# A list scheduler that breaks ties by a table, one number per operation

## The chip, the cores and the metric

The kernel runs on one core of a Trainium2 chip. The metric is the device time of one execution, in microseconds. The engines are named as in the profile: PE is TensorE (PEld its weight loads), DVE is VectorE, ACT is ScalarE, POOL is GpSimd, and SP is SyncE, whose queue issues nearly all DMAs.

## What is computed

A trunk of two layers on 256 tokens of 1024 features, in float32. Each layer normalises x, scales and shifts it by vectors that come from a condition c, mixes, and adds the gated result to x. The first mixer has three attentions whose results are summed under gates: over compressed keys, over selected blocks, and over a window; the second is causal attention.

```python
def reference(x, c, positions, ...):
    cos, sin = rope_tables(positions)
    cond = jax.nn.silu(c)
    for i in range(DEPTH):                      # 2
        shift, scale, gate = jnp.split(cond @ ada_w[i] + ada_b[i], 3, axis=-1)
        h = rms_norm(x, norm_g[i]) * (1 + scale[:, None, :]) + shift[:, None, :]
        y = nsa_mixer(h, ...) if i == 0 else moba_mixer(h, ...)
        x = x + gate[:, None, :] * y
    return x
# both mixers: h @ w_in, norm and rotary embedding of q and k, attention of 16 heads
# (4 of k and v, 64 wide), then (o * silu(z)) @ w_out
```

## The kernel before

The kernel doesn't issue its instructions where they are written. Proxies record each call (`record`): an operation has a number in the order of recording (`id`), an engine, the operations that it depends on, the tiles that it needs, a planned cost, and a `level`. Calls inside `plan.group()` are one operation. At the end `issue` runs a list schedule over the 2447 operations: for each engine it looks for the operation that can start first by the planned times, and issues instructions in the order in which they are picked. Every engine then runs its own instructions in that fixed order, each waiting for what it needs. So a planned time only decides an order.

Among operations of one engine that can start at the same planned time, the one with the smallest (`_rank`, `id`) is taken. The levels are FIRST_OF_ALL = -2 and URGENT = -1 (the norms and what the first products wait for), CHAIN = 0 (attention steps, loads and most else), and FILL = 1 (products with weights, and the splitting of weights). Matmuls that address a part of PE's array (`tile_position`) have rank TILED = -0.5 when the matmul before them was tiled as well. An operation of negative rank may also be taken when it is ready within 250 ns (`AHEAD`). DMAs are operations too: those on SP are recorded with level CHAIN, and a load can be picked as soon as its tag has a free buffer (`room`, `_safe`). There are twelve buffers `early` for the weights of the start, five `raw` for later ones.

Work: a float32 product is made of three fp32r matmuls, of high and low parts: ACT rounds a weight tile of 128 x 1024 to `hi`, DVE takes the rest to `lo`, and the activations stand in `HT` (for products with w_in) or in `qg` tiles (with w_out), split in the same way. `product` issues hi*hi, hi*lo and lo*hi, with 512 or 256 columns. At the start c and x are loaded; `condz` (from c) times `ada_w` in tiled matmuls gives scale and shift (`AB`); x is squared, scaled (`n_in`), transposed on PE, copied from PSUM (`n_out`), and scaled and shifted into `HT`. The first products are those of k and v, k-slice by k-slice, as the slices of HT come. Then come the rest of the first mixer's projections, the compressed keys (`hid`, `pcT`, `kcm`), the attention of eight pairs of heads (scores into `ps`, softmax on DVE and ACT, transposes, `values` in tiled matmuls) with the products of z beside it, the product with w_out, the second norm (`next_h`), and the same for the second mixer.

The last operations to be named in the prediction: 0 is the load of c on ACT's queue, 1 and 2 are the loads of the two halves of x on SP's queue, 22 and 23 the first two pieces of `ada_w` (shift and scale), 24, 25, 28 and 29 the first pieces of `nsa_w_in` (29 has 256 columns), 520 a weight of the compressed keys, 650 to 656 the DVE and ACT steps behind `hid`, and 693 and 694 the `hi` and `lo` of a weight tile that is split at the same time.

Of the kernel before, what the change touches and what calls it, by code (L numbers as in the profile page):

```python
# [36 lines left out]
TILED, LATER = -0.5, 0  # L37
SHORT_ROWS = 1.4
# [13 lines left out]
class Plan:  # L52
# [59 lines left out]
    def _new(self, engine):  # L112
        op = {"id": len(self.ops), "engine": engine, "calls": [], "deps": set(), "needs": set(), "cost": 0.0,
              "level": self.level, "end": None, "columns": 0.0}
        self.ops.append(op)
        return op
# [56 lines left out]
    def _cost(self, engine, method, args, kw, aps):  # L173
# [13 lines left out]
        if engine == "T":  # L187
            if method == "transpose":
                return 262.0 if aps[1].dtype == F32 else 180.0
            cols = free(aps[2])  # L190
            if aps[2].dtype == F32:
                m = free(aps[1])
                if "tile_position" in kw and m <= 64:
                    return max(cols * 4.28 * max(32, m) / P, 60.0)
                return 2 * max(cols * 2.14, 264.0)
            return max(cols * (1.07 if aps[2].dtype == F32R else 1.0), 264.0)
# [22 lines left out]
    @staticmethod  # L219
    def _rank(op, e, mode):  # L220

        if e == "T" and op["level"] >= 0 and op["mode"] and mode:
            return TILED
        if e == "T" and op["mode"] and op["level"] > 0:
            return op["level"] + LATER
        return op["level"]

    def issue(self, opening=()):

        ops = self.ops  # L230
        after = [[] for _ in ops]
        first, last = {}, {}
        for op in ops:
            op["wait"] = len(op["deps"])
            for d in op["deps"]:
                after[d].append(op["id"])
            for name in op["needs"]:
                self.tiles[name]["left"] += 1
                first.setdefault(name, op["id"])
                last[name] = op["id"]  # L240
        for t in self.tags.values():
            t.tiles = sorted((n for n in t.tiles if n in first), key=lambda n: first[n])
            for k, n in enumerate(t.tiles):
                self.tiles[n]["place"] = k
            t.first, t.last = [first[n] for n in t.tiles], [last[n] for n in t.tiles]
            t.alive = [[a for a in range(b + 1) if t.last[a] >= t.first[b]] for b in range(len(t.tiles))]
            assert all(len(a) <= t.bufs for a in t.alive), (t.name, max(map(len, t.alive)), t.bufs)
            t.given, t.early, t.done, t.known = set(), set(), set(), {}
        closed = {}
        for waiting, for_, call in opening:  # L250
# [4 lines left out]
        gates = [g for g in {id(g): g for g in closed.values()}.values()]  # L255

# [18 lines left out]
        for op in ops:  # L275
            op["at"] = 0.0
            if not op["wait"]:
                ready[op["engine"]].append(op)
        done = 0
        while done < len(ops):  # L280
            best = None
            for e, ops_e in ready.items():
# [4 lines left out]
                for op in ops_e:  # L287
# [12 lines left out]
                    found.append((t, self._rank(op, e, mode), op["id"], op))  # L300
# [10 lines left out]
            ready[e].remove(op)  # L311
            for n in op["needs"]:
                t = self.tiles[n]
                if t["slot"] is None:
                    tag = t["tag"]
                    gate = closed.get(tag.name)
                    if gate and not gate["called"]:
                        gate["called"] = True
                        gate["call"]()
# [37 lines left out]
            for a in after[op["id"]]:  # L357
# [3 lines left out]
                if not b["wait"]:  # L361
                    ready[b["engine"]].append(b)
            for method, args, kw in op["calls"]:
                r = getattr(self.engines[e], method)(*[self._real(a) for a in args],  # L364
                                                     **{k: self._real(a) for k, a in kw.items()})
            done += 1
        return max(clock.values())
# [1052 lines left out]
```

## Time and profile before

| what | us |
|---|---|
| three runs | 332.24, 332.68, 333.10 |
| median | 332.68 |
| span of the profiled execution | 329.4 |
| median less span | 3.28 |
| PE busy in the span | 315.2 |

The profiled execution has no time of its own beside its span in what the runs left; the median of the three runs stands 3.28 us over the span. The span runs from the first to the last instruction of the program. Busy times of PE are modelled at their ends: a matmul's row holds waits of the pipeline too, so a stretch in which PE is always busy need not be one in which it works at its full rate. All recorded instructions stand on one line, L364, where they are issued, so tiles tell them apart.

### The profile page before, as it was taken

Reading aid. Unit: us, or ns where it says so; the run is one execution under the profiler, and the core shown is the slowest. Engines: PE = TensorE matmul, PEld = TensorE weight load, DVE = VectorE, ACT = ScalarE, POOL = GpSimd, SP = SyncE. Lnnn points to the kernel's source line nnn. Section 1 sums busy time; section 2 is a strip of 40 time slices with the busy share of each in tenths; the row PEclk is TensorE's granted clock in tenths of the full one; section 3 lists DMA queues with packets and bytes.
Section 4 is the critical chain, followed back from the end, with each engine's and each line's share of the span. In section 5 each row is a group of like instructions: output and inputs, shape, how many; then the busy total and the mean of one; then the engine's idle time right before and its main releaser. Section 6 shows DMA issues by size and latency. Waiting matters only on the chain.

```text
span 329.4 us, 6082 instructions
## 1 busy us (share of the span) xinstructions
PE 315.2 (96%) x2183; PEld 252.8 (77%) x2183; DVE 241.3 (73%) x581; ACT 199.9 (61%) x476; POOL 26.1 (8%) x98
## 2 busy tenths in 40 slices
PE   1989999999989999999999999998999999999995
PEld 1856766888668788768897578866788998989884
DVE  3352543887699899639998665998599999974754
ACT  5542250762674798556776774698565897965420
POOL 7000008950000000000000000000000000000000
PEclk9999999999999999999999999999999999999999
DMA  8998999029896809738455799626386413033102
GB/s 254 336 357 299 375 363 332 5 80 278 271 337 217 290 29 314 262 91 357 129 215 182 243 307 317 209 64 199 119 258 181 141 64 129 0 102 103 54 32 96
DMA packets 43738, 65.80 MB, mean 200 GB/s; under 512 B 3786, under 2 KB 20537, under 8 KB 43708
## 3 DMA queue, kind: packets, MB, share of 16 engines
q1 hardware_dynamic: 43540, 65.36, 60.1%
q8 instruction: 17, 0.28, 0.3%
q14 instruction: 13, 0.11, 0.1%
q10 hardware_dynamic: 168, 0.06, 0.1%
HBM read 64.36 MB, written 1.05 MB: 199 GB/s over the span
## 4 chain that ended last, share of the span: by engine, by line
PE 89%; DVE 3%; ACT 2%; issue 0%; ACTq 0%
PE ps L364 51%; PE acc L364 38%; DVE lo L364 1%; ACT HT L364 1%; DVE rs L364 1%; ACT n_out L364 0%; ACT n_in L364 0%; ACT hi L364 0%; DVE g L364 0%; DVE HT L364 0%; DVE y L364 0%; DVE pcT L364 0%; DVE X L364 0%; ACT pcT L364 0%; DVE n_in L364 0%
## 5 line engine op out<-in xcount | busy, mean ns | idle before, releaser
L364 DVE TENSOR_TENSOR lo<-raw,hi 128x1024 fp32r<-128x1024 f32 (+1 forms) x50 | 59.2, 1186 | 21.4 <-ACT hi L364 21.2
L364 ACT CAST hi<-raw 128x1024 fp32r<-128x1024 f32 (+1 forms) x50 | 51.0, 1025 | 34.5 <-PE acc L364 18.5
L364 PE MATMUL acc<-hi,HT 128*128 128x512 f32 (+1 forms) x176 | 54.1, 382 | 1.3 <-ACT HT L364 0.7
L364 PE MATMUL acc<-HT,hi 128*128 128x256 f32 x256 | 54.3, 297 | 0.0
L364 ACT ACTIVATE p<-ps,tiny 128x128 f32<-128x128 f32 (+1 forms) x96 | 39.5, 433 | 13.6 <-DVE tiny L364 13.4
L364 PEld LDWEIGHTS acc<-HT,hi 128*128 128x128 f32 x256 | 40.9, 189 | 1.4 <-issue 0.9
L364 PEld LDWEIGHTS acc<-hi,HT 128*128 128x128 f32 x176 | 32.0, 188 | 8.5 <-ACT HT L364 1.5
L364 PE MATMUL acc<-HT,lo 128*128 128x256 f32 x128 | 36.7, 287 | 0.0
L364 PE MATMUL acc<-lo,HT 128*128 128x512 f32 (+1 forms) x88 | 33.5, 388 | 0.2 <-DVE lo L364 0.2
L364 DVE TENSOR_REDUCE tiny<-ps 128x2 f32<-128x512 f32 (+2 forms) x40 | 24.8, 630 | 10.0 <-PE ps L364 9.5
L364 PE MATMUL ps<-KTA,qg 128*128 128x256 f32 (+1 forms) x192 | 31.0, 296 | 0.2 <-ACT pcT L364 0.2
L364 PEld LDWEIGHTS ps<-KTA,qg 128*128 128x128 f32 x192 | 25.9, 190 | 4.1 <-issue 2.2
L364 PE MATMUL ps<-hi,HT 128*128 128x512 f32 (+1 forms) x96 | 28.7, 365 | 0.0
L364 PEld LDWEIGHTS acc<-HT,lo 128*128 128x128 f32 x128 | 24.2, 189 | 0.5 <-issue 0.4
L364 ACT COPY pT<-ps 128x384 f32<-128x384 f32 x48 | 21.7, 490 | 3.7 <-PE ps L364 2.9
L364 PE MATMUL ps<-hi,qg 128*128 128x256 f32 (+1 forms) x96 | 23.7, 321 | 0.0
L364 PE MATMUL acc<-hi,qg 128*128 128x512 f32 x64 | 22.2, 397 | 0.0
L364 PE MATMUL ps<-identF,p 128*128 128x128 f32 x144 | 21.5, 275 | 0.0
L364 ACT ACTIVATION_READ_ACCUMULATOR p<-ps,tiny 128x1 f32 x96 | 20.7, 215 | 0.0
L364 PEld LDWEIGHTS acc<-lo,HT 128*128 128x128 f32 x88 | 16.5, 188 | 5.0 <-DVE lo L364 1.1
L364 PEld LDWEIGHTS ps<-hi,HT 128*128 128x128 f32 x96 | 17.1, 188 | 4.1 <-issue 1.6
L364 PE MATMUL ps<-pT,VA 128*64 128x256 f32 (+1 forms) x192 | 18.9, 334 | 0.0
(199 smaller groups left out, 576.4 us busy)
## 6 DMA issues: line engine op xcount, KB each, us to landing
raw<-in_ada_w_dram SPq DMA_DIRECT2D x32, 512.0 KB, 4.8
raw<-in_moba_w_in_dram SPq DMA_DIRECT2D x20, 512.0 KB, 4.0
early<-in_ada_w_dram SPq DMA_DIRECT2D x16, 512.0 KB, 6.8
early<-in_nsa_w_in_dram SPq DMA_DIRECT2D x12, 512.0 KB, 8.7
raw<-in_nsa_w_in_dram SPq DMA_DIRECT2D x12, 512.0 KB, 4.6
raw<-in_nsa_cmp_w_dram SPq DMA_DIRECT2D x8, 512.0 KB, 6.6
raw<-in_nsa_w_out_dram SPq DMA_DIRECT2D x8, 512.0 KB, 5.8
raw<-in_moba_w_out_dram SPq DMA_DIRECT2D x8, 512.0 KB, 3.6
```

Of the source, the lines that this page charges most:

```text
L364: r = getattr(self.engines[e], method)(*[self._real(a) for a in args], **{k: self._real(a) for k, a in kw.items()})
```

## The change

The diff adds a table `TURNS` with one number for each of the 2447 operations, a permutation of 0 to 2446 indexed by the operation's number. The list schedule takes (`_rank`, turn) in place of (`_rank`, number), and all levels above 0 rank as 0. The planned durations of some matmuls change: fp32r products, float32 matmuls, and transposes of 16-bit or fp32r tiles. The schedule is split into `_prepare`, `_order` and `issue`, which by itself changes nothing in what is issued. No operation is added or removed, and the buffers are the same. The table is cut to its first four lines here.

```diff
--- before.py
+++ after.py
@@ -1,3 +1,4 @@
+import collections
 from contextlib import ExitStack, contextmanager
 
 import concourse.bass as bass
@@ -35,6 +36,128 @@
 
 TICK = 10240 / 3
 TILED, LATER = -0.5, 0
+TURNS = [
+    153, 132, 129, 88, 134, 157, 243, 380, 730, 202, 247, 2134, 2043, 1895, 1989, 1464, 1700, 1836, 2107, 352, 282,
+    112, 8, 136, 138, 118, 140, 142, 160, 100, 705, 687, 121, 539, 114, 469, 331, 693, 920, 936, 1244, 1406, 883, 429,
+    526, 742, 574, 600, 1057, 783, 869, 1146, 711, 810, 1130, 774, 905, 533, 908, 1144, 843, 1284, 1152, 492, 1137,
+    1206, 189, 602, 152, 547, 468, 1107, 2241, 2109, 2251, 1794, 1763, 1527, 1788, 2093, 1986, 2242, 1561, 1854, 1652,
...
+    2426, 2442, 2387, 2444, 2430, 2417, 2432, 2425, 2416, 2428, 1147, 1451, 270,
+]
 SHORT_ROWS = 1.4
 ISSUE, FIRST_BYTE, RATE, LANDED = 450.0, 1500.0, 330.0, 700.0
 
@@ -111,7 +234,7 @@
 
     def _new(self, engine):
         op = {"id": len(self.ops), "engine": engine, "calls": [], "deps": set(), "needs": set(), "cost": 0.0,
-              "level": self.level, "end": None, "columns": 0.0}
+              "level": self.level, "end": None}
         self.ops.append(op)
         return op
 
@@ -186,14 +309,14 @@
         n = max(free(a) for a in aps)
         if engine == "T":
             if method == "transpose":
-                return 262.0 if aps[1].dtype == F32 else 180.0
+                return 262.0 if aps[1].dtype == F32 else 204.0
             cols = free(aps[2])
             if aps[2].dtype == F32:
                 m = free(aps[1])
                 if "tile_position" in kw and m <= 64:
-                    return max(cols * 4.28 * max(32, m) / P, 60.0)
-                return 2 * max(cols * 2.14, 264.0)
-            return max(cols * (1.07 if aps[2].dtype == F32R else 1.0), 264.0)
+                    return max(cols * 4.05 * max(32, m) / P, 60.0)
+                return 2 * max(cols * 2.05, 264.0)
+            return max(cols * 1.07 + 9.0 if aps[2].dtype == F32R else cols, 268.0)
         if engine == "A":
             return 0.833 * n + (51.0 if psum else 94.0) + 93.0 * sum(isinstance(kw.get(k), bass.AP) for k in ("bias", "scale", "accum_out"))
         if engine == "G":
@@ -221,21 +344,19 @@
 
         if e == "T" and op["level"] >= 0 and op["mode"] and mode:
             return TILED
-        if e == "T" and op["mode"] and op["level"] > 0:
-            return op["level"] + LATER
-        return op["level"]
-
-    def issue(self, opening=()):
+        return min(op["level"], 0)
+
+    def _prepare(self, opening):
 
         ops = self.ops
-        after = [[] for _ in ops]
+        self.after = [[] for _ in ops]
         first, last = {}, {}
+        self.uses = collections.Counter()
         for op in ops:
-            op["wait"] = len(op["deps"])
             for d in op["deps"]:
-                after[d].append(op["id"])
+                self.after[d].append(op["id"])
             for name in op["needs"]:
-                self.tiles[name]["left"] += 1
+                self.uses[name] += 1
                 first.setdefault(name, op["id"])
                 last[name] = op["id"]
         for t in self.tags.values():
@@ -245,14 +366,26 @@
             t.first, t.last = [first[n] for n in t.tiles], [last[n] for n in t.tiles]
             t.alive = [[a for a in range(b + 1) if t.last[a] >= t.first[b]] for b in range(len(t.tiles))]
             assert all(len(a) <= t.bufs for a in t.alive), (t.name, max(map(len, t.alive)), t.bufs)
+        self.opening = opening
+
+    def _order(self):
+
+        ops = self.ops
+        for op in ops:
+            op["wait"], op["at"] = len(op["deps"]), 0.0
+        for name, t in self.tiles.items():
+            t["left"], t["slot"], t["end"] = self.uses[name], None, 0.0
+        for t in self.tags.values():
+            t.free, t.next = [(0.0, k) for k in range(t.bufs)], 0
             t.given, t.early, t.done, t.known = set(), set(), set(), {}
         closed = {}
-        for waiting, for_, call in opening:
+        for waiting, for_, call in self.opening:
             left = sum(len(self.tags[f].tiles) for f in for_)
             gate = {"left": left, "for": set(for_), "end": 0.0, "call": call, "called": False}
             for w in waiting:
                 closed[w] = gate
         gates = [g for g in {id(g): g for g in closed.values()}.values()]
+        steps = []
 
         def room(name):
 
@@ -273,11 +406,9 @@
         tally, mode = {}, None
         ready = {e: [] for e in self.engines}
         for op in ops:
-            op["at"] = 0.0
             if not op["wait"]:
                 ready[op["engine"]].append(op)
-        done = 0
-        while done < len(ops):
+        while len(steps) < len(ops):
             best = None
             for e, ops_e in ready.items():
                 if not ops_e:
@@ -297,7 +428,7 @@
                         t = max(t, r)
                     if blocked:
                         continue
-                    found.append((t, self._rank(op, e, mode), op["id"], op))
+                    found.append((t, self._rank(op, e, mode), op["turn"], op))
                     first = t if first is None else min(first, t)
                 pick = min(found, key=lambda f: f[:3]) if found else None
                 if pick:
@@ -309,6 +440,7 @@
                     best = pick + (e,)
             start, _, _, op, e = best
             ready[e].remove(op)
+            opens = []
             for n in op["needs"]:
                 t = self.tiles[n]
                 if t["slot"] is None:
@@ -316,7 +448,7 @@
                     gate = closed.get(tag.name)
                     if gate and not gate["called"]:
                         gate["called"] = True
-                        gate["call"]()
+                        opens.append(gate["call"])
                     slot = min(tag.free)
                     tag.free.remove(slot)
                     t["slot"] = slot[1]
@@ -354,17 +486,28 @@
                         if t["tag"].name in g["for"]:
                             g["left"] -= 1
                             g["end"] = max(g["end"], t["end"])
-            for a in after[op["id"]]:
+            for a in self.after[op["id"]]:
                 b = ops[a]
                 b["at"] = max(b["at"], end if e == b["engine"] == "T" else seen)
                 b["wait"] -= 1
                 if not b["wait"]:
                     ready[b["engine"]].append(b)
+            steps.append((op, opens))
+        return max(clock.values()), steps
+
+    def issue(self, opening=()):
+
+        self._prepare(opening)
+        for op in self.ops:
+            op["turn"] = TURNS[op["id"]] if TURNS else op["id"] + 10000 * max(op["level"], 0)
+        end, steps = self._order()
+        for op, opens in steps:
+            for call in opens:
+                call()
             for method, args, kw in op["calls"]:
-                r = getattr(self.engines[e], method)(*[self._real(a) for a in args],
-                                                     **{k: self._real(a) for k, a in kw.items()})
-            done += 1
-        return max(clock.values())
+                getattr(self.engines[op["engine"]], method)(*[self._real(a) for a in args],
+                                                            **{k: self._real(a) for k, a in kw.items()})
+        return end
 
     def _real(self, a):
```

## Rows read from the trace of the kernel before

**Rows 1.** The page: the span, its first part (busy time of each engine, share of the span, instructions), and of its second part the line of what the DMA engines moved in each of 40 equal slices of 8.2 us.
```profile
span 329.4 us, 6082 instructions
...
PE 315.2 (96%) x2183; PEld 252.8 (77%) x2183; DVE 241.3 (73%) x581; ACT 199.9 (61%) x476; POOL 26.1 (8%) x98
...
GB/s 254 336 357 299 375 363 332 5 80 278 271 337 217 290 29 314 262 91 357 129 215 182 243 307 317 209 64 199 119 258 181 141 64 129 0 102 103 54 32 96
```

**Rows 2.** Busy time in stretches of 10 us. Columns: the stretch, its length, then busy us and instructions of PE, PEld, DVE, ACT and POOL, the granted clock of TensorE, the DMA share and GB/s.
```profile
0.00:10.00 10.00, 2.92 (x12) 2.59 (x13) 4.80 (x25) 4.40 (x7) 6.08 (x33) 1.00 0.86 271
10.00:20.00 10.00, 9.80 (x85) 7.39 (x84) 3.96 (x10) 6.49 (x10) 0.00 (x0) 1.00 1.12 338
20.00:30.00 10.00, 9.11 (x76) 5.75 (x74) 3.24 (x8) 1.11 (x2) 0.00 (x0) 1.00 0.94 321
...
90.00:100.00 10.00, 9.18 (x49) 6.79 (x46) 9.90 (x33) 6.20 (x10) 0.00 (x0) 1.00 0.92 316
...
220.00:230.00 10.00, 8.99 (x42) 6.43 (x42) 9.39 (x22) 8.64 (x24) 0.00 (x0) 1.00 0.50 158
...
320.00:330.00 10.00, 5.75 (x37) 5.00 (x35) 4.47 (x8) 0.00 (x0) 0.00 (x0) 0.95 0.25 92
sum 330.00, PE 315.23 PEld 252.81 DVE 241.27 ACT 199.91 POOL 26.14; mean PE 9.55 PEld 7.66 DVE 7.31 ACT 6.06 POOL 0.79
```

**Rows 3.** The chain that ended last, in stretches where PE is fed. Columns: start in us, how long, whose work, how many instructions (x24 on `ps` are matmuls with 256 columns, x12 on `acc` with 512).
```profile
208.55 2.84 PE ps L364 x24
211.40 2.79 PE acc L364 x12
```

**Rows 4.** The same chain in the attention of the first mixer. The `ps` pieces of two and three instructions are transposes or other matmuls of 110 ns.
```profile
138.02 1.38 PE acc L364 x12
139.40 0.86 PE ps L364 x2
140.25 0.35 PE acc L364 x3
140.61 0.33 PE ps L364 x3
...
158.33 0.36 PE acc L364 x3
158.69 0.52 PE ps L364 x2
```

**Rows 5.** Instructions in order of time around two holes of PE. Columns: start, how long, engine, line, operation, tile written and tiles read, shapes, count, and in brackets the idle time before it and what ended it.
```profile
91.66 0.49 PE L364 MATMUL acc<-hi,HT 128*128 128x512 f32 x1 [0.59 <-ACT n_in L364]
92.39 0.51 PE L364 MATMUL acc<-lo,HT 128*128 128x512 f32 x1 [0.23 <-DVE lo L364]
...
224.26 0.40 PE L364 MATMUL acc<-hi,HT 128*128 128x512 f32 x1
225.66 0.75 PEld L364 LDWEIGHTS ps<-identF,n_in 128*128 128x128 f32 x6 [1.44 <-DVE n_in L364]
```

**Rows 6.** In order of time, the first issues of SP's queue (SPq; the duration is that of issuing).
```profile
0.80 0.85 SPq L364 DMA_DIRECT2D X<-in_x_dram  x2
1.69 1.78 SPq L364 DMA_DIRECT2D early<-in_ada_w_dram  x2
4.35 2.54 SPq L364 DMA_DIRECT2D early<-in_nsa_w_in_dram  x2
```

**Rows 7.** DMA issues by line: how many, KB each, median us from issue to landing.
```profile
X<-in_x_dram SPq DMA_DIRECT2D x2, 512.0 KB, 4.5
```

**Rows 8.** In order of time, what stands before the first product: the load of `c`, `condz` made from it, the second half of the scaled x, its copy from PSUM, HT, and the first product.
```profile
0.79 0.59 ACTq L364 DMA_DIRECT2D rot<-in_c_dram  x1
...
4.99 0.17 DVE L364 TENSOR_TENSOR condz<-sg,RT 128x8 f32<-128x8 f32 x1
...
9.59 0.48 DVE L364 TENSOR_SCALAR n_in<-X,rs 128x512 f32<-128x512 f32 x1
...
12.77 1.07 ACT L364 COPY n_out<-ps 128x512 f32<-128x512 f32 x2 [0.83 <-PE ps L364]
...
15.56 0.60 ACT L364 ACTIVATE HT<-n_out,AB 128x256 fp32r<-128x256 f32 x1 [0.18 <-DVE AB L364]
...
16.21 0.73 PE L364 MATMUL acc<-hi,HT 128*128 128x512 f32 x2 [0.20 <-ACT HT L364]
```

**Rows 9.** In order of time, PE's first and last stretch of tiled matmuls (`condz` with 32 columns of weights, `pT` with 64) and two between, with what follows them.
```profile
10.63 1.51 PE L364 MATMUL ps<-early,condz 128*32 128x128 f32 x16
...
272.42 0.87 PE L364 MATMUL ps<-pT,VA 128*64 128x256 f32 x8
273.23 0.97 PE L364 MATMUL ps<-identR,n_parts 128*128 128x128 f32 x9
...
288.78 1.52 PE L364 MATMUL ps<-pT,VA 128*64 128x256 f32 x16
290.23 0.74 PE L364 MATMUL ps<-KTA,qg 128*128 128x256 f32 x4
...
297.00 0.87 PE L364 MATMUL ps<-pT,VA 128*64 128x256 f32 x8
```

115 rows, old and new, of the table TURNS are left out of this document.

## The prediction

> **What bounds the kernel now.** I read the page first. TensorE (PE) is busy 315.2 us of a span of 329.4 us, 96%, VectorE (DVE) 73%, ScalarE (ACT) 61% [rows 1]. The change issues the same instructions, so PE's own work stays: what an order can win is PE's idle time, and waits that hide inside "busy" rows. The Trainium skill (Perfetto Trace Analysis, Identifying the Most-Contended Engine) says that matmul busy share is a poor measure of TensorE's headroom and that the LDWEIGHTS share should be taken; by that share, 77% here, 76 us would be open instead of 14. The sum below goes by idle time and by measured waits instead.
>
> The stages show where the idle time lies [rows 2]. Of 14.2 us (329.4 - 315.2), 7.08 fall in the first 10 us, before loads have landed, and 3.65 after the last matmuls (9.4 - 5.75: the last eviction, the update of X, the store). An order of ready work hardly reaches the latter. In between stand 0.20 and 0.89 us in 10 to 30, 0.82 in 90 to 100, 1.01 in 220 to 230, and 0.53 in all other stages together (the rest of 14.2). So at most 3.5 us of visible idle time is open.
>
> Then the chain that ended last, for what "busy" hides. Where PE is fed, 12 matmuls with 512 columns take 2.79 us (232 ns each) and 24 with 256 columns 2.84 us (118 ns) [rows 3]. In the attention stages the same chain shows steps that cost more than their work: three transposes take 0.33 us there, so two should take 0.22, but take 0.86 at 139.40 and 0.52 at 158.69 [rows 4]: 0.64 and 0.30 us of waiting inside a busy engine, 0.47 on average. Attention fills eleven of the 10-us stages (120 to 190 and 260 to 300). At one such wait for each, an estimate, 5.2 us are hidden there.
>
> **The change, part by part.**
>
> (1) The durations of TensorE. No instruction comes or goes; they only move the planner's clock. A 512-column matmul goes from 228 to 232 ns (547.8 and 556.8 cycles at 2.4 GHz), which is what the chain shows [rows 3]. Cost nothing by itself; it makes the plan's times for PE truer.
>
> (2) Rank. All levels from 0 up now count as 0, so a product (FILL) and an attention step (CHAIN) that could start at the same time are told apart by the table. Read against the operations, the table still puts PE's attention steps (mostly under 1000) before its products (mostly 1300 to 2400), and ACT's and DVE's weight splits late (693 and 694 have 2290 and 2403). So chain before fill stays the rule, and what changes is the order among chain steps and among products. Negative levels still come before everything.
>
> (3) The start. This is where the table visibly moves something. All loads into free buffers are ready at once on SP, so their turns are their order. Now SP issues X (two halves), then the two ada_w pieces, then weights [rows 6]. By the table (operation numbers count from 0): 22 (ada_w, turn 8), 29 (w_in, 256 columns, 100), 25 (w_in, 118), then X (2 and 1: 129 and 132), then 23 (the other ada_w piece, 136). X is put behind 0.52 + 0.26 + 0.52 = 1.3 MB, and the second ada_w piece behind 0.78 MB more than now. At the 254 and 336 GB/s of the first two slices [rows 1] X lands 3.9 to 5.2 us later and that piece 2.3 to 3.1 us later. Now X is issued at 0.80 and lands 4.5 us later, at 5.3 [rows 6, 7]; the second half of the scaled x is done at 10.07 and its copies from PSUM end at 13.84, HT starts at 15.56 and the first product at 16.21 [rows 8]. The stretch from landing to 10.07 is 4.8 us of squares and small DVE steps; with transposes and two copies at about 0.55 us each right behind, an estimate of 7.0 us to the end of the copies. So X later by 4.4 gives copies at 5.3 + 4.4 + 7.0 = 16.7, and with HT (0.6) the first product at about 17.4, 1.2 later than now. If the ada_w piece decides instead, the first tiled matmuls (10.63 now [rows 9]) and all behind them shift by up to 3.1. Below nothing is excluded for this term: no input of the first product that decides lands earlier. I take +1.2, ends 0 and +3.1. From 30 us on PE shows no idle time, so such a delay reaches the end, less what 10 to 30 absorbs (next term). On ACT's queue c goes from first to third, some 0.6 us later for each load ahead (its own issue takes 0.59 [rows 8]); condz is made from it at 4.99 now and first used at 10.63 [rows 8, 9], so 5 us cover it: nothing. Without that cover it would cost 1.2 us.
>
> (4) The idle 1.09 us of 10 to 30 us [rows 2]. Weights now land before they can be used, so that PE should go on without a hole once started. I take half, -0.5; ends 0 and -1.1.
>
> (5) The other idle time, 2.36 us (0.82, 1.01, 0.53). At 91.66 and 92.39 PE waits for an eviction and a weight split [rows 5], and that split stands behind the chain of the compressed keys on DVE in the new table as well (2403 against 398 to 797). At 224 it runs dry while the small steps of the second norm end [rows 5], which have negative levels and which the table doesn't reach. So I take a quarter, -0.6; ends 0 and -2.4. What comes late next at both places is the same split on DVE.
>
> (6) The tiled matmuls (those that address a part of the array). There are 54 groups in the code and I count 32 stretches, from 10.63 to 297.00 [rows 9]. Eight matmuls take 0.81 us (272.42 to 273.23), sixteen in one stretch 1.45 (288.78 to 290.23), so joining two stretches saves 0.17 us and splitting one costs it. The planner still prefers a tiled group right after another. Two or three more joins, -0.4; ends +0.8 (five splits) and -1.7 (ten joins).
>
> (7) The hidden waits, 5.2 us. The table can reach these, since it sets which product stands between two steps of a chain. But many of them end with ACT or DVE, whose work and planned durations are unchanged and which are 61 and 73% busy, in bursts. I take 40%, -2.1; ends 0 and -5.2.
>
> (8) Order on SP and POOL behind the start: POOL works 26.1 us in all [rows 1], most of it early, and nothing is queued long behind it. On SP later loads change places too (520, a weight of the compressed keys, has 291 where those behind it have 251 to 264), but five buffers let only the next few go ahead. Cost nothing, hidden by products of the pieces already in. If a piece came late, its product would wait as at 92.39, 0.2 us; this lies within the ends of (5).
>
> **Sum:** +1.2 - 0.5 - 0.6 - 0.4 - 2.1 = -2.4 us. Against the profiled execution: span 329.4 - 2.4 = 327.0, and the 3.3 us that lie around it (median 332.68 less span) stay: 330.3 us, 0.7% below the median.
>
> **The rivals.**
>
> *The start costs more than the order wins (slower).* Place: the first product on HT. X and the second ada_w piece land later by the loads put before them, and PE has nothing else. Price: +3.1, and half of the gains of (4) to (7), -1.8: 334.0. It decides once the first product starts later than about 19.3 us. For it: SP's order in the table, and a PE without idle time afterwards to absorb it. Against it: 1.7 us of slack between the copies of x (13.84) and HT (15.56) now [rows 8]. Chance 0.19.
>
> *Tiled groups are torn apart (slower).* If the turns put products between groups, all 22 joins of now are lost: 22 x 0.17 = 3.7 us, and with the rest of the sum 332.7 - 2.0 + 3.7 = 334.4. Against it: the rank for tiled groups stays. The Trainium skill (TensorEngine Tiling, Key Properties) says that a change of tiling mode drains the array; the 0.17 us agree with it in sign. Chance 0.04.
>
> *No change that can be told.* The table only speaks among operations that can start at the same time, and chain stays before fill; a PE that is 96% busy then does the same work in another order, and waits move rather than go. The start and the hidden waits cancel: 332.7. Chance 0.16.
>
> *Much more goes.* Of the 10.4 us that all bounds of (4) to (7) hold together, 60% goes and the start costs nothing: 332.7 - 6.2 = 326.5. For it: the waits are many and small, which order can fill. Against it: DVE's bursts. Chance 0.18.
>
> **How the numbers follow.** The forecast has 0.43. A difference of 0.3%, 1.0 us, is about what a measurement here can tell from none. Faster: 0.43 + 0.18, less a little of the forecast's near side, 0.60. Same: 0.16 and that little, 0.17. Slower: 0.23. The range goes from the large gain, 326.5, to the late start with fewer gains than above (3.1 - 1.2: 334.6); outside it lie the rest of both ends, 2 in 10.
>
> **What the changed profile would show.** (3) SP's first load is ada_w, X lands at about 9.7 us, and the first product on HT starts at about 17.4. Right if 16.2 to 18; the first rival if over 19.3. (4) PE idle in 20 to 30 us under 0.5. (5) The holes at 90 and at 224 still there, somewhat shorter. (6) About 30 tiled stretches. (7) Fewer steps of two matmuls that take over 0.5 us in attention; the stages from 30 us to the end shorter by about 3. PE's busy time should fall with the span, since hidden waits lie in it. What would make it wrong: a first product that starts no later than now, or a total that moves through idle time that I count as out of reach, the first 10 us or the tail.

## The result and the profile after

The changed kernel takes 327.51 us (median of 4 runs, 327.35 to 328.55) against 332.81 us of the kernel before (4 runs, 332.24 to 333.10). The ratio is 0.9861, interval 0.9834 to 0.9889: 1.4% faster. The profiled execution of after has a span of 325.8 us and a time of its own of 327.62, so 1.82 us lie around its span. Before's later executions, with time and span side by side, have 2.0 to 2.1 us around it (332.04 with 330.0, 331.69 with 329.6), and spans from 329.2 to 332.1. The profiled one of before, 329.4, is at the low end of these, so the spans differ by 3.6 us and the medians by 5.3. The two traces explain the 3.6.

The page of after answers [rows 1]. PE's busy time fell with the span, by 3.0 us; the engine is still busy for 96%.

```profile
span 325.8 us, 6076 instructions
...
PE 312.2 (96%) x2183; PEld 251.5 (77%) x2183; DVE 241.9 (74%) x581; ACT 199.9 (61%) x476; POOL 26.5 (8%) x98
...
GB/s 235 330 358 364 361 371 287 13 115 320 277 250 259 272 199 179 325 312 231 171 125 152 249 333 240 256 66 141 118 256 160 165 67 66 129 66 68 63 0 129
```

The stages of after, columns as in [rows 2]. PE starts later (1.98 us busy in the first ten instead of 2.92) and then has no idle time at all from 10 to 30. The hole at 90 is gone and another stands at 80 to 90 (0.69). At the second norm 1.16 us are idle in 210 to 230 (1.27 in before).

```profile
0.00:10.00 10.00, 1.98 (x16) 1.52 (x18) 2.60 (x9) 3.87 (x5) 6.06 (x33) 1.00 0.79 260
10.00:20.00 10.00, 10.00 (x86) 8.38 (x84) 6.93 (x26) 6.59 (x13) 0.00 (x0) 1.00 1.13 333
20.00:30.00 10.00, 10.00 (x81) 6.73 (x78) 2.91 (x8) 2.19 (x4) 0.00 (x0) 1.00 1.08 364
...
80.00:90.00 10.00, 9.31 (x70) 7.27 (x66) 5.37 (x12) 7.86 (x15) 0.00 (x0) 1.00 0.91 294
90.00:100.00 10.00, 9.98 (x53) 6.87 (x52) 9.61 (x29) 5.04 (x9) 0.00 (x0) 1.00 0.81 259
...
210.00:220.00 10.00, 9.48 (x43) 6.72 (x42) 8.54 (x22) 8.68 (x22) 0.00 (x0) 1.00 0.20 63
220.00:230.00 10.00, 9.36 (x44) 6.86 (x43) 7.13 (x19) 6.83 (x17) 0.00 (x0) 1.00 0.53 158
```

The start of after in order of time answers [rows 6] and [rows 8]: two kinds of weights are issued ahead of X; two weight tiles are split (`hi`, `lo`) while X is still landing; the squares wait for X at 9.18 and 10.52; the copies end at 16.65; HT starts at 16.68. One more tiled stretch stands ahead of the first product at 17.95.

```profile
0.79 0.42 SPq L508 DMA_DIRECT2D early<-in_ada_w_dram  x1
1.27 1.09 SPq L508 DMA_DIRECT2D early<-in_nsa_w_in_dram  x2
3.70 1.49 SPq L508 DMA_DIRECT2D X<-in_x_dram  x2
...
6.46 0.60 ACT L508 CAST hi<-early 128x512 fp32r<-128x512 f32 x1
7.92 1.04 ACT L508 CAST hi<-early 128x1024 fp32r<-128x1024 f32 x1 [0.86 <-DMA early<-in_nsa_w_in_dram]
8.54 1.83 DVE L508 TENSOR_TENSOR lo<-early,hi 128x512 fp32r<-128x512 f32 x2
9.18 1.06 ACT L508 ACTIVATE n_in<-X 128x1024 f32<-128x1024 f32 x1 [0.21 <-DMA X<-in_x_dram]
...
15.57 1.08 ACT L508 COPY n_out<-ps 128x512 f32<-128x512 f32 x2 [0.97 <-PE ps L508]
16.68 0.60 ACT L508 ACTIVATE HT<-n_out,AB 128x256 fp32r<-128x256 f32 x1
16.95 1.07 PE L508 MATMUL ps<-early,condz 128*32 128x128 f32 x16
17.95 0.50 PE L508 MATMUL ps<-hi,HT 128*128 128x512 f32 x1
```

**Where the 3.6 us went.** Both kernels issue the same matmuls, so they can be compared at equal work. I give each matmul the duration that the changed planner has for it (293.1 us in all), and take the time at which a given amount of it has been started, less that amount: the time lost by then. Each difference between two columns is what is lost in between. The point of 8 us of work is passed at about 21 us, 40 at about 57, 80 at about 100, 200 in the second norm.

| us of work done | 8 | 20 | 40 | 80 | 200 | all |
|---|---|---|---|---|---|---|
| before | 12.42 | 15.30 | 17.84 | 21.44 | 29.99 | 32.46 |
| after | 13.81 | 14.59 | 16.67 | 19.71 | 27.17 | 28.86 |
| after less before | +1.39 | -0.71 | -1.17 | -1.73 | -2.82 | -3.60 |

So after stands 1.4 us behind at first and gets 2.1 us back at once; then it wins 0.5 us each from 20 to 40 and from 40 to 80, 1.1 up to the second norm (0.4 of it in the hole before that norm's transposes) and 0.8 in the second mixer. A single pair of profiles gives such a column only roughly: e10 and e11 below have the same two orders with one buffer more, and their last row would be +2.1, 0.0, -0.4, -1.8, -2.7, -3.0. What holds in both pairs is the 2.1 us between 8 and 20.

What it gets back at once is seen in the order of time of PE in before, at 20 to 24 us: after a tiled stretch PE has nothing until DVE has copied `row`, and the products in hand end before the second slice of HT is there.

```profile
20.45 1.07 PE L364 MATMUL ps<-early,condz 128*32 128x128 f32 x16
21.92 0.38 PE L364 MATMUL ps<-selP,row 128*128 128x2 f32 x2 [0.39 <-DVE row L364]
...
23.37 0.50 PE L364 MATMUL acc<-hi,HT 128*128 128x512 f32 x1 [0.50 <-ACT HT L364]
```

In after a product stands behind that stretch while the row is copied, and more products behind `selP`, all on weights that are split already. Nothing waits:

```profile
19.54 1.07 PE L508 MATMUL ps<-early,condz 128*32 128x128 f32 x16
20.54 0.51 PE L508 MATMUL acc<-lo,HT 128*128 128x512 f32 x1
21.00 0.38 PE L508 MATMUL ps<-selP,row 128*128 128x2 f32 x2
21.25 0.47 PE L508 MATMUL acc<-hi,HT 128*128 128x512 f32 x1
21.56 0.40 PE L508 MATMUL acc<-lo,HT 128*128 128x512 f32 x1
```

### The profile page after: what moved, and what is told of

Same layout as the page of the kernel before. It is cut to its first block, busy times and chain, and to the rows that moved or that the text cites. A ratio compares the mean times of both kernels' runs of the same rounds, so it can differ in the third digit from the quotient of the medians.

```text
span 325.8 us, 6076 instructions
## 1 busy us (share of the span) xinstructions
PE 312.2 (96%) x2183; PEld 251.5 (77%) x2183; DVE 241.9 (74%) x581; ACT 199.9 (61%) x476; POOL 26.5 (8%) x98
## 4 chain that ended last, share of the span: by engine, by line
PE 91%; DMA 3%; ACT 2%; DVE 2%; ACTq 1%; issue 1%; SPq 0%
PE ps L508 53%; PE acc L508 37%; DMA raw<-in_nsa_w_in_dram 2%; DMA y<-in_nsa_cmp_pe_dram 1%; ACTq L508 1%; ACT n_out L508 1%; DVE rs L508 1%; ACT HT L508 0%; ACT y L508 0%; ACT n_in L508 0%; DVE lo L508 0%; ACT hi L508 0%; DVE n_out L508 0%; DVE y L508 0%; DVE HT L508 0%
## 5 line engine op out<-in xcount | busy, mean ns | idle before, releaser
L508 PE MATMUL acc<-hi,HT 128*128 128x512 f32 (+1 forms) x176 | 54.8, 383 | 0.0
L508 PE MATMUL acc<-HT,hi 128*128 128x256 f32 x256 | 51.8, 291 | 0.0
L508 ACT ACTIVATE p<-ps,tiny 128x256 f32<-128x256 f32 (+1 forms) x96 | 39.9, 438 | 11.0 <-DVE tiny L508 10.7
L508 PEld LDWEIGHTS acc<-HT,hi 128*128 128x128 f32 x256 | 40.1, 188 | 2.5 <-issue 1.8
L508 PE MATMUL acc<-HT,lo 128*128 128x256 f32 x128 | 37.4, 297 | 0.0
L508 PE MATMUL ps<-KTA,qg 128*128 128x256 f32 (+1 forms) x192 | 30.0, 294 | 0.0
L508 PEld LDWEIGHTS ps<-identF,p 128*128 128x128 f32 x144 | 16.2, 141 | 3.9 <-issue 1.8
```

Of the source, the lines that this page charges most:

```text
L508: getattr(self.engines[op["engine"]], method)(*[self._real(a) for a in args], **{k: self._real(a) for k, a in kw.items()})
```

## The experiments

### Durations without the table, and the table without the durations

e1 takes the table out of after (the rank and the durations stay); e2 takes the old durations with the table (the other changed lines of durations go back too).

```diff
# e1, against after
-TURNS = [
-    153, 132, 129, ...
-]
+TURNS = []
# e2, against after
-                return 262.0 if aps[1].dtype == F32 else 204.0
+                return 262.0 if aps[1].dtype == F32 else 180.0
...
```

> The new durations of TensorE and the new rank, with the table empty: ties are broken by level and number as before. Theory A (the table's order over many small waits gives the gain): no gain, 332 to 335 us, since the durations alone move the plan's clock by 2% on TensorE and its order by chance. Rival C (a plan made with truer durations is the gain, and the table is chance): 327 to 329 us. In between, 330: both share.

> The table with TensorE's durations as before. Theory A': the table only breaks ties at planned times, so it belongs to the durations that it was made with; with others the ties fall elsewhere and the gain is lost: slower than the kernel before, 335 to 345 us. Rival (the table holds a better order of priorities as such, whatever the plan's clock): 327 to 330 us.

e1: 340.22 us, ratio 1.0182 (1.0134 to 1.0230). e2: 355.76 us, ratio 1.0674 (1.0641 to 1.0708). Neither half is a gain, and both lie above the bands that I had set; the durations alone cost 1.8%, and the table with the old durations 6.7%. A table of turns speaks only among operations that are ready together on the planner's clock, so another clock turns it into another order. The two parts belong together. Each of the two runs also pays at the second norm, where PE is left without work; e2 in stretches of 2 us (PE busy, granted clock, DMA share, GB/s):

```profile
228.00:230.00 2.00, 0.52 (x3) 1.00 0.48 129
230.00:232.00 2.00, 0.00 (x0) 0.91 0.60 222
232.00:234.00 2.00, 0.41 (x2) 0.50 0.00 0
...
236.00:238.00 2.00, 2.00 (x5) 0.50 0.00 0
```

### The start's loads and splits

These kernels issue an order that is written out, instead of the one the schedule finds (`SEQ` holds the 2447 numbers in order):

```diff
+            if SEQ:
+                op = ops[SEQ[len(steps)]]
...
# e3: after's order with X (1, 2) first on SP and c (0) first on ACT
+SEQ = [1, 2, 0] + [x for x in AFTER if x > 2]
# e4: before's order with 22, 29, 25 ahead of X
# e12: e3's order, on ACT  98, 82, 31, 30 -> 31, 30, 98, 82
#      and on DVE the low parts 99, 83 -> behind 48, 55
```

> The changed kernel's order of every engine, but SP's first two issues are the loads of X again, and ACT's first load is c. My step on the start: the first product starts earlier by the 1.7 us that the change put it back (17.95 to about 16.2 to 16.9), and PE without idle time behind it carries most of it to the end: 0.8 to 1.5 us faster than the changed kernel, 326.0 to 326.7. Rival B (putting the weights and ada_w ahead of X is part of the gain): slower than the changed kernel by 1 us or more, 328.5 to 330.

> The order of before on every engine, but SP issues the ada_w piece 22 and the weight pieces 29 and 25 ahead of X, as the changed kernel does. My step on the start: the first product starts 1.2 to 3.1 us later than 16.2, and the whole is 0.5 to 2.5 us slower than before (333.3 to 335.3). Rival B: faster than before by 1 us or more.

> The order of after once more with X's two loads first on SP's queue and c's first on ScalarE's, as in e3, but the two early splits that e3 left ahead of the squares (casts of w_in of 128x512 and 128x1024 on ScalarE, their low parts on VectorE) now stand behind the squares and behind the two row scalings; nothing else is moved. It computes the same. First theory (what the start wins is that TensorE's products stand behind a stock of split weights, so that it doesn't run dry between 18 and 42 us; where X stands is a price of about a microsecond that could be had back): the first product comes at 15.8 to 16.8, as early as in the kernel before (16.21), the early splits done by about 14, and the time is 326.0 to 327.3, at or below after's 327.5. Rival (the loads decide: with X's 1 MB ahead of them the weights land later, whatever the engines' order, and e3 lost its 1.7 us there): first product again earlier than in after, but TensorE then waits for splits or loads behind it, and the time is that of e3, 328.5 to 329.8. Third (start positions of single instructions no longer matter, since TensorE is bound by later work): within 0.5 of 327.5 though the first product comes over 1 us earlier.

e4: 335.65 us, ratio 1.0086 (1.0057 to 1.0115), first product at 20.50. X put late in the order of before costs 3 us and gives nothing back: there two matmuls on X stand near the head of PE's order, and PE waits 8.41 us for X before them. So the loads' order by itself is not what wins.

e3: 329.19 us, ratio 0.9891 (0.9867 to 0.9915), 1.7 us slower than after by the medians (1.0 by the ratios, whose intervals overlap), and the first product at 18.68 is later still. So my step on the start (326.0 to 326.7) missed, and the rival's 328.5 to 330 held. X landed early, but nobody was free for it. On ACT the two casts, which stand ahead of the squares, now wait for their loads, and the squares come at 10.79:

```profile
8.48 0.62 ACT L524 CAST hi<-early 128x512 fp32r<-128x512 f32 x1 [3.92 <-DMA early<-in_nsa_w_in_dram]
9.84 1.04 ACT L524 CAST hi<-early 128x1024 fp32r<-128x1024 f32 x1 [0.74 <-DMA early<-in_nsa_w_in_dram]
10.79 1.05 ACT L524 ACTIVATE n_in<-X 128x1024 f32<-128x1024 f32 x1
```

e12: 330.01 us, ratio 0.9923 (0.9897 to 0.9948), slower than after; from e3 the intervals don't tell it apart. The squares do start at 5.70, but the next step on DVE stands behind a copy that waits 5.70 us for PE, which transposes a small input that is there at about 8.0. PE's order still has tiled stretches and 16 matmuls on X (tiles `X` and `identF`; they write a tile that no operation reads) ahead of the transposes of `n_in`. And HT waits for AB, whose steps now stand on DVE behind the two low parts. The first product comes at 18.31.

```profile
5.70 1.06 ACT L524 ACTIVATE n_in<-X 128x1024 f32<-128x1024 f32 x1 [1.14 <-DMA X<-in_x_dram]
8.55 0.26 DVE L524 COPY RT<-ps 128x100 f32<-128x100 f32 x1 [5.70 <-PE ps L524]
15.49 1.82 DVE L524 TENSOR_TENSOR lo<-early,hi 128x512 fp32r<-128x512 f32 x2
17.66 0.60 ACT L524 ACTIVATE HT<-n_out,AB 128x256 fp32r<-128x256 f32 x1 [1.11 <-DVE AB L524]
18.31 0.50 PE L524 MATMUL ps<-hi,HT 128*128 128x512 f32 x1 [0.40 <-ACT HT L524]
```

The first theory of e12 fell, since the first product came nowhere near 16; but the test was not a clean one, since the low parts, done at 17.3 instead of 10.4, hold up the first product by themselves (0.40 us of PE), and a cast costs PE another 0.28 at 19.79. On the time the rival was the nearer one (330.0 against 328.5 to 329.8). As it has it, the weights land later than in after: the first two casts start at 8.4 and 9.8 us in e12 and e3, after waiting for their loads, and at 6.46 and 7.92 in after. But the first product was not earlier, as it also said. What the early splits are worth by themselves is not shown.

### Which stage gives how much

e5 issues the first 560 operations as before does and the rest as after; e6 the reverse. e7 and e8 cut at 1400, about where the attention of the first mixer ends. The first 560 hold 62 us of PE's planned work (to about 80 us on the chip), the first 1400 hold 168.

```diff
# e5 (e6 with the two exchanged; e7 and e8 with 1400)
+SEQ = BEFORE[:560] + [x for x in AFTER if x not in BEFORE[:560]]
```

> On every engine the first 560 operations in the order of the kernel before (to about 65 us: the loads, norm and products of k and v), then all others in the changed kernel's order. Theory A (gain behind the start): 327 to 328.5 us, since the start cost 0.7 us more by my sum. Theory B (the start as a whole is part of the gain, since the loads and the order on ACT and PE there fit each other): slower than the changed kernel by 1 us or more, 328.5 to 330.

> The mirror: the first 560 operations as in the changed kernel, then all others in the order of before. Theory A: no gain or a loss, 332.5 to 333.5. Theory B: 330.5 to 331.7.

> The first 1400 operations (to the end of the first mixer's attention, about 190 us) in the order of before, the rest in the changed kernel's. Theory A says that most hidden waits lie in attention: of the gain of 5.3 us about half comes before this cut (3.5 by my terms of seven attention stages against four), so 329.5 to 330.5. Rival D (the gain lies late, in the change of layers and in the second mixer): 327.5 to 328.7. Rival E (all of it lies before the cut): 332 or more.

> The mirror: the first 1400 operations as in the changed kernel, the rest in the order of before. Theory A: 329 to 330.5. Rival D: 331.5 or more. Rival E: 327.5 to 328.5. If the parts add up, the gains of this run and of its mirror sum to 5.3 us.

| kernel | us | ratio (interval) | lost at 20 | at 40 | at 80 | at 200 | all |
|---|---|---|---|---|---|---|---|
| e5, start of before | 329.91 | 0.9919 (0.9897 to 0.9941) | 15.66 | 18.12 | 22.14 | 29.77 | 31.77 |
| e6, start of after | 330.69 | 0.9937 (0.9916 to 0.9959) | 13.88 | 15.94 | 20.70 | 29.55 | 32.12 |
| e7, before up to the end of attention | 334.33 | 1.0040 (1.0022 to 1.0057) | 16.62 | 19.08 | 23.40 | 33.97 | 35.71 |
| e8, after up to the end of attention | 329.95 | 0.9915 (0.9894 to 0.9936) | 14.84 | 16.90 | 20.68 | 28.72 | 31.42 |

After's start wins about 2 us whichever way it is taken: e5 is 2.4 us above after, e6 2.5 below its runs of before (333.21). The traces agree up to 40 us of work (15.94, 16.67, 16.90 against 17.84, 18.12, 19.08). At this cut the parts add up: e5, with after's order behind the start, gains 3.3 us on its runs of before, so the two gain 5.8 together, against 5.3 for the whole change. At the cut of 1400 they don't: e7, which has only the later part of after, loses 1.1 us and e8 gains 3.3, together 2.1. By the bands set before, e8 lies where half of the gain comes before that cut, and e7 where all of it does. Both can't be so: the seam itself costs about 3 us. In e7's profile 10.6 us are lost between 80 and 200 us of work, against 8.6 in before and 7.5 in after; what waits there is not shown.

### The tiled stretches

e9 is after's order with 15 of its joins split, each by one product moved between two tiled groups: 29 stretches become 44.

```diff
# e9, against after's order: for each of 15 pairs of adjacent tiled groups (p, q)
-  ..., product, ..., p, q, ...
+  ..., ..., p, product, q, ...
```

> The changed kernel's order, but fifteen of the tiled groups that follow another tiled group get one product put between them on PE: 44 tiled stretches in place of 29. My step on tiled groups: 0.17 us for each split, 15 x 0.17 = 2.6 us slower than the changed kernel, 330.1. Rival (a split costs a drain at either end, and the product put there is late for its own readers): 4 us or more, over 331.5. Rival (PE hides it): 327.5 to 328.3.

332.50 us, ratio 0.9998 (0.9979 to 1.0018): 5.0 us above after, all of its gain. That is 0.33 us for each split, twice the 0.17 that I had, and past the 4 us of the rival. One of after's stretches of 16 in order of time, and a split one in e9:

```profile
299.28 1.52 PE L508 MATMUL ps<-pT,VA 128*64 128x256 f32 x16
300.73 0.39 PE L508 MATMUL acc<-HT,hi 128*128 128x256 f32 x1
```

```profile
303.26 0.87 PE L524 MATMUL ps<-pT,VA 128*64 128x256 f32 x8
304.06 0.38 PE L524 MATMUL acc<-HT,lo 128*128 128x256 f32 x1
304.37 0.87 PE L524 MATMUL ps<-pT,VA 128*64 128x256 f32 x8
305.17 0.39 PE L524 MATMUL acc<-HT,hi 128*128 128x256 f32 x1
```

From start to start the whole stretch takes 1.45 us; the two halves take 0.80 each, and the product between them 0.31, where it takes 0.118 in a fed stretch [rows 3]. So a split costs 1.60 - 1.45 + 0.31 - 0.118 = 0.34 us, and 15 of them 5.1.

### One buffer more

In the first 50 us of before the DMAs slow down once (299 GB/s in the fourth slice of [rows 1], where after has 364; 273 in 28 to 32 us). e10 and e11 give the early weights a thirteenth buffer, in the order of before and of after.

```diff
-    plan.tag("early", early["pool"], 1024, 12)
+    plan.tag("early", early["pool"], 1024, 13)
```

> The order of before on every engine, with 13 buffers for the first weights in place of 12. Theory F (the first 56 us are bound by the stream of loads; before, it falls to 273 GB/s between 28 and 32 us while SP waits for a buffer that the tiled matmuls hold, and the changed kernel's gain in the start is that it doesn't): the dip goes, the last tiled matmuls on early weights end about 1.2 us sooner (56.9 to 58.2 in three profiles of that start), and the whole is 1 to 1.8 us faster than before, 331 to 332. Rival G (the start is bound by PE's order, by which products stand ready): no change, 332.6 to 333.3.

> The changed kernel's order with 13 buffers for the first weights. Theory F: its stream already runs at 355 to 374 GB/s from 16 to 52 us, so a buffer more has nothing to give: 327.2 to 327.9. Rival G': the stream or the splits still wait for buffers, so that it gains as much as before does: 326.0 to 326.7.

e10: 332.59 us, ratio 1.0001 (0.9983 to 1.0020). e11: 327.53, ratio 0.9862 (0.9835 to 0.9888). In e10 the dip gets smaller (324 GB/s in 28 to 32 us), and neither time moves: what the start wins is not room for loads. That leaves the order on the engines.

## Why the prediction was right, and where it wasn't

The sign and the size were right: -2.4 us of span predicted, -3.6 measured between the profiles, and 327.51 us lies within the range, 2.8 below the forecast. Of these 2.8, the sum was short by 1.2, and 1.5 is what lies around the span: I carried 3.28 us over, but that was about 2.0 and a profiled execution that was faster than the median.

(1) **Durations.** "Cost nothing by itself" was wrong: in e1 they change the order, and without the table that costs 1.8%, some 6 us. In the sum this didn't show, since here they come with the table.

(2) **Rank.** Not tested by a run of its own; nothing in the traces speaks against it.

(3) **The start.** The dates held, the path only in part. X's squares wait for its landing at 9.18 and 10.52 (I had 9.7), the copies end at 16.65 (16.7), HT starts at 16.68, and the first product comes at 17.95 instead of 16.21 (I had 17.4; the missing 0.55 us is a tiled stretch that is put ahead of it). At 8 us of work after is 1.39 us behind; the term was +1.2. But the chain that ended last doesn't pass through X:

```profile
2.81 4.60 DMA y<-in_nsa_cmp_pe_dram
7.99 0.26 DVE RT L508
8.66 10.49 PE ps L508 x86
```

A small load on ACT's queue, for the compressed keys, lands at 7.41. Its copy stands on DVE ahead of the steps to condz, so that condz is made at 8.44 (4.99 in [rows 8]) though c itself was there at 5.86; the first tiled matmuls wait for it, and from 8.66 to the first product PE has no idle time. I had costed the later c at nothing, with 5 us of cover; the cover is gone. X is close behind this path but not on it: the last part of the scaled x is ready at 15.68 for transposes that start at 15.95, and before that it stood on DVE behind a copy that waited 0.68 us for PE. e3 and e12 show that X put first doesn't bring the first product forward. So that 17.4 came near is in part luck. One reading of mine was off as well: ACT ends the last part of the scaled x at 11.94 in before, not at 10.07.

PE's own rate matters on this path, and I had not looked at it. The same 16 tiled matmuls take 1.92 us at 8.66 and 1.07 at 16.95, and 16 matmuls on X, whose result nothing reads, take 3.44: 0.213 us each up to about 13.4 and 0.11 behind, as at 1.2 and 2.4 GHz.

```profile
8.66 1.92 PE L508 MATMUL ps<-early,condz 128*32 128x128 f32 x16 [0.71 <-DVE condz L508]
10.51 3.44 PE L508 MATMUL ps<-X,identF 128*128 128x128 f32 x16
```

The rows of these stretches give a granted clock of 1.00, but the trace has a record of it only from 13.45 us on (from 11.59 in before), and the rate doubles there. This time differs between profiles of the same start, and the first product with it. In e6 the record begins at 11.82 and in e11 at 15.20; the same matmuls on X take 2.61 and 3.79 us, and the first product comes at 17.23 and 18.92, with X's first squares at 8.90 and 9.10:

```profile
10.62 2.61 PE L524 MATMUL ps<-X,identF 128*128 128x128 f32 x16
10.84 3.79 PE L524 MATMUL ps<-X,identF 128*128 128x128 f32 x16
```

The time lost at 8 us of work runs from 13.1 to 14.8 us in the five profiles with after's start, so one pair of profiles doesn't give the +1.39 to better than about 1 us.

(4) **The idle time of 10 to 30: the step that failed.** I gave it half of what stood idle, -0.5, and -1.1 at most. The idle time went entirely, and with it waits inside busy rows: from 8 to 20 us of work before loses 2.88 us and after 0.78, which is -2.1, and -0.5 more up to 40. The start as a whole therefore came out at -1.2 in the profiles, about -2 in e5 and e6, not at +0.7. My step said that weights land before they can be used; what counts is that some are split by then, and that the order puts a product behind each wait. The rows of 19.54 to 21.56 show it; that it is the whole of the gain is not shown (e12).

(5) **Other idle time.** Predicted -0.6, measured -0.4 (2.36 to 1.96). The hole at 90 is gone and another stands at 82, where PE waits for ACT's `y`, which stands behind a cast that waits for its load (8); the one before the second norm's transposes fell from 1.01 to 0.64 us:

```profile
80.73 0.70 ACT L508 CAST hi<-raw 128x608 fp32r<-128x608 f32 x1 [4.31 <-DMA raw<-in_nsa_w_in_dram]
81.34 1.13 ACT L508 COPY y<-n_out 128x512 f32<-128x512 f32 x2
82.01 1.18 PE L508 MATMUL ps<-identF,y 128*128 128x128 f32 x8 [0.69 <-ACT y L508]
...
223.00 1.50 PE L508 MATMUL ps<-identF,n_in 128*128 128x128 f32 x8 [0.64 <-DVE n_in L508]
```

(6) **Tiled stretches.** 32 became 29: three joins, as predicted, all in the second mixer, where six stretches of 8 and one of 16 became four of 16. The price was wrong by half: I had taken two stretches against one and left out their neighbours. Three joins at 0.34 are -1.0, which is about all that the second mixer wins (-0.8; -0.3 between e10 and e11, where e11 has a hole of 0.36 there). The Trainium skill (TensorEngine Tiling, Key Properties) says that a change of mode drains the array. The traces agree in that a change of mode costs time, 0.34 us here for the two of a split; that a drain is the cause they don't show. By that price the rival of torn groups would have cost 7.5 us and not 3.7.

(7) **Hidden waits.** Predicted -2.1. Outside the start and the joins, the table of lost time leaves -0.6 (40 to 80 us of work, with the hole of (5)) and -1.1 (80 to 200): about -1.3 without (5). The sign I named is wrong: steps of two matmuls of over 0.5 us in attention did not become fewer in the chain; there are two in before, 0.86 and 0.52, and three of 0.86 in after (149.44, 178.75 and 189.59; the first of them here):

```profile
149.44 0.86 PE ps L508 x2
```

Such a row was a poor measure; time lost at equal work is a better one. Which waits went in attention is not shown.

(8) **SP and POOL behind the start.** "Cost nothing" failed in one place. The hole at 82 goes back to a load of `nsa_w_in` that lands at 80.66: ACT's cast waits 4.31 us for it, the copy of `y` stands behind the cast, and PE loses 0.69 us, where I had 0.2 for a late piece. It lies within the ends of (5), as I had said.

So in the sum +1.2 and -0.6 held, -0.5 was about 2 too small, -0.4 was half of what it should be, and -2.1 was too large. That the total came within 1.2 us is in part luck: these errors partly cancel. Of the rivals, "the start costs more" had the mechanism (first product later) but not its condition (over 19.3); e4, with 20.50, shows its price, 3 us, in an order that doesn't fit. "Much more goes" is nearest on the time (326.5), but by another road: the start did cost its 1.2 us. The Trainium skill (Perfetto Trace Analysis, Identifying the Most-Contended Engine) would have me judge headroom by MFU (the share of peak that the matmuls reach) and the LDWEIGHTS share. That share is 77% before and after, though 3.6 us of the span went, so it didn't measure what was won here.

What stays open: why e12 and e3, with after's order behind the start, lose 11.3 and 12.0 us between 40 and 200 us of work where after loses 10.5. No experiment separates this. Nor does any run leave out the matmuls on X, which take 3.4 us of the path to the first product in after. No version tried is faster than after.

## What to carry to other kernels

Judge a reordering by time lost at equal work, not by idle time: a busy engine hides waits, and a later start can be paid back within some 15 us if ready work stands behind each wait. Before a late start is put down to a late load, compare the rate of the first matmuls with that of the same ones later. Price the change of a mode with its neighbours, by the start-to-start times of the whole stretch. And an order, its planned durations and its loads fit one another: half of such a change says little about the whole, and can be a loss (e1, e2, e7).

## What had not been expected of the hardware

- One product between two tiled stretches costs 0.34 us, of which 0.19 lies in the product itself (0.31 instead of 0.118 us for 256 columns).
- In e2 the granted clock fell from 1.00 to 0.50 (from 2.4 to 1.2 GHz) at about 231.6 us, after PE had been busy for 0.52 us of four, and stayed there until about 238.4, while PE was busy again from 233.6 on. Eight transposes took 1.97 us there; the same take 1.10 at 14.88 in after. After's shorter hole at the same place (0.64 us) left the clock at 1.00.
- The same order starts differently from run to run, since PE works at half its rate at first and that ends at different times: at 11.8 to 15.2 us in the five profiles with after's start (after, e6, e8, e9, e11), at 11.6 to 14.1 in the four with before's (before, e5, e7, e10). The first product comes at 17.23 to 18.92 and at 16.21 to 17.58. In e11 the small load that DVE waits for is later as well, but only by 0.32 us (PE takes it at 7.87, in after at 7.55), of 0.97 us at the first product. The runs of before spread from 331.24 to 334.12 us; how much of that comes from the start is not shown.
